# Two layers of attention on one core: the opening's instructions re-ordered, with 14 turns of the identity ahead of the first product

## The chip, the cores and the metric

The kernel runs on one core of a Trainium2 chip. The core has five engines with an instruction queue each: TensorE (matrix products into PSUM; PE in the profile, PEld for its weight loads), VectorE (DVE), ScalarE (ACT), GpSimd (POOL) and SyncE (SP, which here only issues transfers). Each works through its own queue in order, and an instruction that waits holds up all that is queued behind it on its engine. The metric is the device time of one execution in microseconds; lower is better.

## What is computed

Two layers over 1024 latent tokens and 256 context tokens of width 1024: layer 0 with windowed attention, layer 1 with latent attention. The change concerns the first steps of layer 0: the adaLN vector, the norm of every token, and the product with the columns of `w_in` that give the values.

```python
m = jax.nn.silu(cond) @ w + bias               # shift, scale, gate of the layer
hx = rms_norm(x, norm_g[i]) * (1.0 + scale_x[:, None]) + shift_x[:, None]
hc = rms_norm(ctx, norm_g[i]) * (1.0 + scale_c) + shift_c
q, k, v, g = jnp.split(h @ w_in, [...], axis=-1)
```

After the second layer the latent tokens go through a last `rms_norm`. All is in 32-bit floats; a product is made of three TensorE products, with each operand split in a top half (`hi`, rounded) and what is left (`lo`): hi with hi, hi with lo, lo with hi.

## The kernel before

**The opening** (lines 822 to 1056) makes `hT`, the normed, scaled and turned tokens, and at once multiplies them with the first block of `w_in` (`wt[0]`, the values). It cuts the 1280 tokens in five parts `p` of 256 (0 is the context) and the width of 1024 in four quarters `b` of 256, that is two `k` of 128 each. A *group* is a pair (p, b). `groups` lists their order: (0,0), (1,0), (2,0), (0,1), (1,1), (2,1), (3,0), (3,1), (4,0), (4,1), then all parts of quarters 2 and 3.

The order is written out by hand: the block is a `manual_schedule`, so every engine takes its instructions in the order of the code, and a step can't overtake another on its engine. (The planner `Plan`, which orders later stages by costs and due times, isn't on here.) The steps, by name:

- `x_load(p)` loads 256 tokens as two halves `j` of 128 (SP). `square(p)` (line 860, ScalarE, one Square with a sum per half), `norm(p)` (line 865, VectorE's mean, then a power of -0.5 on POOL) and `scale(p, j, engine)` (line 870) norm them in place.
- `ada_load(q, kk)`, `ada_mm(q, kk)`, `ada_copy()`, `ada_cols(q)` make the columns of scale and shift (`ada0.A`, `ada0.B`) of quarter q: 256 KB pieces of `ada_w` on SP, small products in the upper left of bank 6 (line 839), a copy by ScalarE (844), two products by `sel` (849), and three additions on VectorE (`set_cols`, 328 to 331). Four buffers hold the pieces, so a load of the next q waits for the `ada_mm` that reads its buffer.
- `turn(p, b, bank)` (line 877): four 128 x 128 transposes on TensorE into bank 5 or 7.
- `h_part(p, b, hi)` (line 884): per k one VectorE instruction (890) takes the bank times A plus B to `h`; then one cast (892) by ScalarE or POOL writes the top half of both k.
- `h_low(p, b, eng)` (line 895): h minus the top half, on VectorE or POOL.
- `v_part(p, b)` (line 899): the group's products: eight with the top half (906), then four with the low half (911), summed in PSUM bank p.
- `w0_load(i)`, `w0_cut(i)` (lines 923, 927): a quarter of `wt[0]`, and its split: top on ScalarE or POOL, low on POOL.
- `make(i)` (line 936): `turn`, `h_part` and `h_low` of group i.

Two buffers hold `h` (`hr`), and `PB` is the whole of PSUM in eight banks: 0 to 4 take the five parts' sums, 3 and 4 the thrown-away squares of parts 0 to 2 as well, 5 and 7 the turns, 6 the adaLN. The opening ends about 70 us after the start with the copies of the values (`v_out`) and the first products of the next block. In the last opening of the kernel, that of layer 1, lines 1464 and 1465 apply scale and shift with ScalarE on one half of a bank and VectorE on the other:

```python
nc.scalar.activation(h[:, 1], ps[:, 1], AF.Identity, bias=sb[:, 1], scale=sa[:, 1])
nc.vector.tensor_scalar(h[:, 0], ps[:, 0], sa[:, 0], sb[:, 0], ALU.mult, ALU.add)
```

Of the kernel before, what the change touches and what calls it, by code (L numbers as in the profile page):

```python
# [14 lines left out]
AF = mybir.ActivationFunctionType  # L15
ALU = mybir.AluOpType
# [4 lines left out]
D = 1024  # L21
# [5 lines left out]
EPS = 1e-6  # L27
# [190 lines left out]
def kernel(ctx: ExitStack, tc: tile.TileContext, t, out, dbg=None):  # L218
    plan = Plan()
    nc = Recorder(tc.nc, plan)  # L220
# [75 lines left out]
    mhalf = sm(1)  # L296
# [538 lines left out]
    def ada_mm(q, kk):  # L835
        for k in range(2):
            for a in range(2):
                r = 64 * k + 32 * a
                nc.tensor.matmul(
                    PA[r : r + 2, 0:256], sc[:, 2 * kk + k, :], aw[q, kk][:, k, a], start=kk == 0, stop=kk == 3  # L840
                )

    def ada_copy():
        nc.scalar.copy(am[0:98], PA[0:98, 0:256])

    def ada_cols(q):
        for j in range(2):
            o = PA[:, 256 + 34 * j : 290 + 34 * j]
            nc.tensor.matmul(o, am[0:98, j * 128 : j * 128 + 128], sel[0:98], start=True, stop=True)
        m = shp(PA[:, 256:512], 2, 34)  # L850
        ada0.set_cols(m[:, :, 32:34], 1, q, 2)
        ada0.set_cols(m[:, :, 0:2], 0, q, 2)
# [4 lines left out]
        for j in range(2):  # L857
            load(out=xn[p][0][:, j], in_=src[j * 128 : j * 128 + 128, :])

    def square(p):  # L860
        junk = V[:, 8:10].rearrange("p a b c -> p (a b c)") if p > 2 else PB[:, 3:5, :].rearrange("p a b -> p (a b)")
        for j in range(2):
            nc.scalar.activation(junk, xn[p][0][:, j], AF.Square, accum_out=xn[p][1][:, j : j + 1])

    def norm(p):
        _, sq, st = xn[p]
        nc.vector.tensor_scalar(st[:, 0:2], sq[:, 0:2], 1.0 / D, EPS, ALU.mult, ALU.add)
        nc.gpsimd.tensor_tensor(st[:, 2:4], st[:, 0:2], mhalf.to_broadcast([128, 2]), ALU.pow)

    def scale(p, j, eng):  # L870
        x, r = xn[p][0][:, j], xn[p][2][:, 2 + j : 3 + j]
        if eng is nc.scalar:
            nc.scalar.activation(x, x, AF.Copy, scale=r)
        else:
            eng.tensor_scalar_mul(x, x, r)

    def turn(p, b, bank):
        tbank[p, b] = ps = shp(PB[:, bank, :], 2, 256)
        for kk in range(2):
            for j in range(2):  # L880
                c0 = (2 * b + kk) * 128
                nc.tensor.transpose(ps[:, kk, j * 128 : j * 128 + 128], xn[p][0][:, j, c0 : c0 + 128], ident)

    def h_part(p, b, hi=nc.scalar.copy):
        w = 1 if p == 0 else 0
        ps, h = tbank[p, b], shp(hr.next(), 2, 256)
        for kk in range(2):
            k = 2 * b + kk
            sa, sb = ada0.A[:, k, w : w + 1], ada0.B[:, k, w : w + 1]
            nc.vector.tensor_scalar(h[:, kk], ps[:, kk], sa, sb, ALU.mult, ALU.add)  # L890
        ks = slice(2 * b, 2 * b + 2)
        hi(hT[p][:, 0, ks, :], h)
        hs[p, b] = h

    def h_low(p, b, eng=nc.gpsimd):
        ks = slice(2 * b, 2 * b + 2)
        eng.tensor_sub(hT[p][:, 1, ks, :], hs[p, b], hT[p][:, 0, ks, :].bitcast(F32))

    def v_part(p, b):
        h, W = hT[p], wt[0]  # L900
        for j in range(2):
            js = slice(j * 128, j * 128 + 128)
            o = PB[:, p, j * 256 : j * 256 + 256]
            for k in (2 * b, 2 * b + 1):
                for s in range(2):
                    nc.tensor.matmul(o, h[:, 0, k, js], W[:, s, k, :], start=k == j == s == 0, stop=False)  # L906
        for j in range(2):
            js = slice(j * 128, j * 128 + 128)
            o = PB[:, p, j * 256 : j * 256 + 256]
            for k in (2 * b, 2 * b + 1):  # L910
                nc.tensor.matmul(o, h[:, 1, k, js], W[:, 0, k, :], start=False, stop=j == 1 and k == 7)
# [15 lines left out]
    def w0_cut(i, top=nc.scalar.copy):  # L927
        hi, lo = (wt[0][:, s, 2 * i : 2 * i + 2, :] for s in range(2))
        top(hi, w0[i])
        nc.gpsimd.tensor_sub(lo, w0[i], hi.bitcast(F32))  # L930
# [5 lines left out]
    def make(i):  # L936
        if i < NG:
            turn(*groups[i], (5, 7)[i % 2])
            h_part(*groups[i], nc.gpsimd.tensor_copy if i == 3 else nc.scalar.copy)
        if i < 9:  # L940
            h_low(*groups[i])
        elif 10 < i <= NG:
            h_low(*groups[i - 1], nc.vector if i % 2 or i in (14, 16) else nc.gpsimd)
        if i == 9:
            h_low(*groups[i])
# [20 lines left out]
    ada_mm(0, 3)  # L966
    ada_copy()
    ada_cols(0)
    for kk in range(4):
        ada_load(1, kk)  # L970
    x_load(3)
    w0_load(2)
    w0_load(3)
    w0_cut(0, nc.gpsimd.tensor_copy)
    h_part(0, 0, nc.gpsimd.tensor_copy)
    square(1)
    norm(1)
    h_low(0, 0, nc.vector)
    for j in range(2):
        scale(1, j, nc.vector)  # L980
    v_part(0, 0)
    turn(1, 0, 7)
    square(2)
    norm(2)
    h_part(1, 0)
    scale(2, 0, nc.vector)
    scale(2, 1, nc.scalar)
    w0_cut(1)
    for kk in range(2):
        ada_mm(1, kk)  # L990
    h_low(1, 0, nc.vector)
    v_part(1, 0)
    turn(2, 0, 5)
    ada_mm(1, 2)
    h_part(2, 0)
    h_low(2, 0, nc.vector)
    ada_mm(1, 3)
    ada_copy()
    turn(0, 1, 7)
    ada_cols(1)  # L1000
    x_load(4)
    for kk in range(4):
        ada_load(2, kk)
    v_part(2, 0)
    turn(1, 1, 5)
    h_part(0, 1, nc.gpsimd.tensor_copy)
    square(3)
    h_low(0, 1, nc.vector)
    norm(3)
    h_part(1, 1)  # L1010
    h_low(1, 1)
    for i in range(3, NG):
        p, q = groups[i]
        if i > 7:
            make(i + 2)
        if i == 3:
            scale(3, 0, nc.vector)
            scale(3, 1, nc.scalar)
        v_part(p, q)
        if i < 8:  # L1020
            make(i + 2)
        if i == 3:
            square(4)
            norm(4)
        if i == 5:
            scale(4, 0, nc.vector)
            scale(4, 1, nc.scalar)
            ada_mm(2, 0)
            ada_mm(2, 1)
            w0_cut(2)  # L1030
        if i == 6:
            ada_mm(2, 2)
            ada_mm(2, 3)
            ada_copy()
            w0_cut(3)
        if i == 7:
            ada_cols(2)
            for kk in range(4):
                ada_load(3, kk)
        if i == 9:  # L1040
            fetch(1)
        if i in (9, 11):
            ada_mm(3, i - 9)
            ada_mm(3, i - 8)
        if i == 11:
            ada_copy()
            load(out=cosa, in_=t["cos_a"])
            load(out=sina, in_=t["sin_a"])
        if i == 12:
            ada_cols(3)  # L1050
        if i > 15:
            v_out(p - 1)
        if i in (12, 14, 16):
            next_item()
# [444 lines left out]
    for k in range(8):  # L1499
        w0_cut1(k, nc.vector if k % 2 else nc.gpsimd)  # L1500
        if k % 2:
            b = k // 2
# [611 lines left out]
```

## Time and profile before

| | |
|---|---|
| runs shown | 1487.2, 1489.08, 1856.97 us; median 1489.08 |
| the profiled execution | 1487.75 us, with a span of 1485.6 us from first to last instruction |
| mean granted TensorE clock | 0.998 |
| the opening: TensorE busy, 0 to 20 us | 8.43 us |
| 20 to 45 us | 23.18 us of 25 |
| DMA queues busy, 10 to 35 us | 1.06 to 1.11 of their 16 engines |

A row of the timeline gives start and length in us from the span's start, engine, line, operation, what it writes and reads, and, in brackets, how long the engine had been idle before it and what ended that. Instructions of one kind in a row are merged (x8). Lengths of TensorE's instructions overlap, as they are pipelined, so its rate is read from start to start. A transpose or a 32-bit product of `ada_mm` may show as more than one record. A row by groups gives busy time, mean length in ns of one, and idle time. A row by stretches gives, per engine (PE, PEld, DVE, ACT, POOL), busy time and instructions, then the granted clock, the DMA share and GB/s.

### The profile page before, as it was taken

Reading aid. Unit: us, or ns where it says so; the run is one execution under the profiler, and the core shown is the slowest. Engines: PE = TensorE matmul, PEld = TensorE weight load, DVE = VectorE, ACT = ScalarE, POOL = GpSimd, SP = SyncE. Lnnn points to the kernel's source line nnn. Section 1 sums busy time; section 2 is a strip of 40 time slices with the busy share of each in tenths; the row PEclk is TensorE's granted clock in tenths of the full one; section 3 lists DMA queues with packets and bytes.
Section 4 is the critical chain, followed back from the end, with each engine's and each line's share of the span. In section 5 each row is a group of like instructions: output and inputs, shape, how many; then the busy total and the mean of one; then the engine's idle time right before and its main releaser. Section 6 shows DMA issues by size and latency. Waiting matters only on the chain.

```text
span 1485.6 us, 25066 instructions
## 1 busy us (share of the span) xinstructions
PE 1462.1 (98%) x9036; PEld 1186.8 (80%) x9036; DVE 1060.5 (71%) x2025; ACT 737.5 (50%) x1401; POOL 808.6 (54%) x735
## 2 busy tenths in 40 slices
PE   6999999999999999999999999999999999999998
PEld 4888888888888888889888888767777767866687
DVE  3787789648778888877988777666576466556764
ACT  4421222359888878877554432443454344444321
POOL 2563366356454444456300240798788788789371
PEclk9999999999999999999999999999999999999999
DMA  9545644573343333337344566011112212120442
GB/s 334 173 166 175 212 146 174 186 245 110 122 140 121 104 100 100 97 98 257 101 118 120 169 236 201 23 44 49 50 61 69 61 47 62 54 68 28 154 148 86
DMA packets 146964, 186.01 MB, mean 125 GB/s; under 512 B 12812, under 2 KB 100492, under 8 KB 146840
## 3 DMA queue, kind: packets, MB, share of 16 engines
q1 hardware_dynamic: 141864, 177.75, 37.9%
q10 hardware_dynamic: 4976, 6.66, 1.3%
q8 instruction: 71, 1.16, 0.3%
q14 instruction: 53, 0.43, 0.1%
HBM read 134.02 MB, written 46.15 MB: 121 GB/s over the span
## 4 chain that ended last, share of the span: by engine, by line
PE 90%; DVE 4%; DMA 2%; issue 1%; ACT 1%; POOL 0%; POOLq 0%; DVEq 0%; ACTq 0%
PE PB L285 14%; PE PB L286 14%; PE PB L287 14%; PE PB L1791 13%; PE PB L1814 9%; PE PB L737 5%; PE PB L1757 5%; PE PB L727 5%; PE PB L697 3%; PE PB L698 3%; DMA arena_f<-ada_w 1%; PE PB L1825 1%; PE PB L906 1%; DVE arena_r L281 1%; PE PB L756 1%
## 5 line engine op out<-in xcount | busy, mean ns | idle before, releaser
L285 PE MATMUL PB<-arena_r 128*128 128x512 f32 (+2 forms) x1200 | 439.4, 366 | 1.1 <-DVE arena_f L1239 1.1
L286 PE MATMUL PB<-arena_r 128*128 128x512 f32 (+2 forms) x1200 | 433.7, 361 | 0.0
L287 PE MATMUL PB<-arena_r 128*128 128x512 f32 (+2 forms) x1200 | 433.3, 361 | 0.0
L1807 POOL TENSOR_TENSOR arena_f<-arena_f 128x1024 f32<-128x1024 f32 x120 | 285.9, 2383 | 8.2
L285 PEld LDWEIGHTS PB<-arena_r 128*128 128x128 f32 x1200 | 226.3, 189 | 45.7 <-issue 9.0
L287 PEld LDWEIGHTS PB<-arena_r 128*128 128x128 f32 x1200 | 226.3, 189 | 33.5
L286 PEld LDWEIGHTS PB<-arena_r 128*128 128x128 f32 x1200 | 226.4, 189 | 32.1 <-POOL arena_r L281 0.6
L1791 PE MATMUL PB<-arena_r 64*128 64x512 f32 (+1 forms) x1600 | 229.3, 395 | 0.0
L1801 ACT ACTIVATE arena_f<-PB 128x1024 f32<-128x1024 f32 x160 | 164.5, 1028 | 111.7 <-PE PB L1791 84.9
L1763 DVE TENSOR_REDUCE krF<-PB 128x1 f32<-128x512 f32 (+1 forms) x264 | 166.9, 677 | 65.6 <-PE PB L1757 65.6
L1791 PEld LDWEIGHTS PB<-arena_r 64*128 64x128 f32 (+1 forms) x1600 | 178.2, 185 | 15.7 <-issue 5.2
L704 DVE CUSTOM_DVE_ANT_0 arena_f<-PB,arena_f,small 128x256 f32<-128x256 f32 (+1 forms) x288 | 148.1, 524 | 51.4 <-PE PB L698 32.8
L280 ACT CAST arena_r<-PB 128x512 fp32r<-128x512 f32 (+2 forms) x207 | 115.3, 563 | 113.2 <-PE PB L287 73.3
L281 DVE TENSOR_TENSOR arena_r<-PB,arena_r 128x512 fp32r<-128x512 f32 (+2 forms) x207 | 134.2, 660 | 35.1 <-ACT arena_r L280 34.4
L1814 PE MATMUL PB<-arena_f 128*64 128x512 f32 x640 | 146.0, 595 | 0.0
L281 POOL TENSOR_TENSOR arena_r<-arena_f,arena_r 128x512 fp32r<-128x512 f32 (+1 forms) x64 | 87.7, 1386 | 105.2 <-ACT arena_r L280 91.0
L280 ACT CAST arena_r<-arena_f 128x512 fp32r<-128x512 f32 (+1 forms) x142 | 82.3, 610 | 90.2 <-PE PB L287 27.8
L710 ACT ACTIVATE arena_f<-arena_f,small 128x640 f32<-128x640 f32 (+2 forms) x160 | 119.1, 745 | 15.8 <-DVE small L704 13.7
L507 DVE SCALAR_TENSOR_TENSOR arena_f<-arena_f,small 128x512 f32<-128x512 f32 x98 | 114.9, 1217 | 10.5 <-DMA arena_f<-ada_w 10.3
L737 PE MATMUL PB<-arena_r 128*128 128x512 f32 x336 | 118.7, 429 | 0.0
L1757 PE MATMUL PB<-arena_r 64*128 64x512 f32 (+1 forms) x768 | 113.9, 355 | 0.1
L727 PE MATMUL PB<-ident,arena_f 128*128 128x128 f32 x672 | 108.7, 272 | 0.1
(216 smaller groups left out, 2083.0 us busy)
## 6 DMA issues: line engine op xcount, KB each, us to landing
arena_f<-ada_w SPq DMA_DIRECT2D x96, 256.0 KB, 4.1
arena_r<-q_d SPq DMA_DIRECT2D x160, 128.0 KB, 2.8
arena_f<-a_w_in SPq DMA_DIRECT2D x40, 256.0 KB, 4.1
arena_f<-b_w_in SPq DMA_DIRECT2D x36, 256.0 KB, 3.3
arena_f<-x SPq DMA_DIRECT2D x16, 512.0 KB, 6.4
q_d<-arena_f SPq DMA_DIRECT2D x16, 512.0 KB, 3.0
arena_r<-qn_d SPq DMA_DIRECT2D x16, 512.0 KB, 5.1
g_d<-arena_f ACTq DMA_DIRECT2D x20, 256.0 KB, 4.1
```

The source lines that it names most:

```text
L280: nc.scalar.copy(hi, src)
L281: (lo_eng or nc.vector).tensor_sub(lo, src, hi.bitcast(F32))
L285: nc.tensor.matmul(o, ah, bh, start=first, stop=False)
L286: nc.tensor.matmul(o, al, bh, start=False, stop=False)
L287: nc.tensor.matmul(o, ah, bl, start=False, stop=last)
L727: nc.tensor.transpose(pt[:, h, :], self.Ps[h][:, ci * 128 : ci * 128 + 128], ident)
L737: nc.tensor.matmul(self.pv, V[:, self.chunks[ci], self.g, :], PT[:, s], start=ci == 0 and s == 0, stop=ci == self.m - 1 and s == 1,)
L1757: nc.tensor.matmul(bank[:, o : o + n], self.q[r, s, bs], k[r, 0, n0 : n0 + n], start=s == 0, stop=s == 2)
L1763: nc.vector.reduce_max(self.mxp[:, e, b : b + 1, i], bank[:, 0:n], AX.X)
L1791: nc.tensor.matmul(PB[:, b + e, :], k[r, s, cs], q[r, sq], start=i == 0, stop=i == 4)
L1807: eng.tensor_add(acc, acc, E)
L1814: nc.tensor.matmul(PB[r, 7, :], Vq[:, c, h, :], E[:, e], start=c == 0, stop=c == NT - 1)
```

## The change

The opening's order is written anew; what is computed stays the same. `square` and `norm` can take one half of a part. `turn` goes half by half (j outside, k inside), `v_part` by k and not by j, so that a group can start when the first k is there. `h_part` gets two more forms: with `hi=None` ScalarE applies scale and shift itself from PSUM to the top half, beside VectorE's own pass; with `parts=2` the cast is made per k. Fourteen turns of the identity into bank 2 stand between `ada_cols(0)` and the first product. Turns of later groups stand ahead of `v_part` of earlier ones, the four `ada_mm(2)` move behind group (3,1), and with them the turns of part 4.

```diff
-    def square(p):
+    def square(p, js=range(2)):
...
-        for j in range(2):
+        for j in js:
...
-    def norm(p):
+    def norm(p, j=0, n=2):
         _, sq, st = xn[p]
-        nc.vector.tensor_scalar(st[:, 0:2], sq[:, 0:2], 1.0 / D, EPS, ALU.mult, ALU.add)
-        nc.gpsimd.tensor_tensor(st[:, 2:4], st[:, 0:2], mhalf.to_broadcast([128, 2]), ALU.pow)
+        nc.vector.tensor_scalar(st[:, j : j + n], sq[:, j : j + n], 1.0 / D, EPS, ALU.mult, ALU.add)
+        nc.gpsimd.tensor_tensor(st[:, 2 + j : 2 + j + n], st[:, j : j + n], mhalf.to_broadcast([128, n]), ALU.pow)
...
     def turn(p, b, bank):
         tbank[p, b] = ps = shp(PB[:, bank, :], 2, 256)
-        for kk in range(2):
-            for j in range(2):
+        for j in range(2):
+            for kk in range(2):
...
-    def h_part(p, b, hi=nc.scalar.copy):
+    def h_part(p, b, hi=nc.scalar.copy, parts=1):
...
             nc.vector.tensor_scalar(h[:, kk], ps[:, kk], sa, sb, ALU.mult, ALU.add)
+            if hi is None:
+                nc.scalar.activation(hT[p][:, 0, k], ps[:, kk], AF.Identity, bias=sb, scale=sa)
+            elif parts == 2:
+                hi(hT[p][:, 0, k], h[:, kk])
         ks = slice(2 * b, 2 * b + 2)
-        hi(hT[p][:, 0, ks, :], h)
+        if hi and parts == 1:
+            hi(hT[p][:, 0, ks, :], h)
...
     def v_part(p, b):
         h, W = hT[p], wt[0]
-        for j in range(2):
-            js = slice(j * 128, j * 128 + 128)
-            o = PB[:, p, j * 256 : j * 256 + 256]
-            for k in (2 * b, 2 * b + 1):
+        for k in (2 * b, 2 * b + 1):
+            for j in range(2):
+                js = slice(j * 128, j * 128 + 128)
+                o = PB[:, p, j * 256 : j * 256 + 256]
...
     def make(i):
         if i < NG:
             turn(*groups[i], (5, 7)[i % 2])
-            h_part(*groups[i], nc.gpsimd.tensor_copy if i == 3 else nc.scalar.copy)
+            h_part(*groups[i])
...
     ada_cols(0)
+    for _ in range(14):
+        nc.tensor.transpose(PB[:, 2, 0:128], ident, ident)
...
-    h_part(0, 0, nc.gpsimd.tensor_copy)
-    square(1)
-    norm(1)
+    h_part(0, 0, nc.gpsimd.tensor_copy, 2)
+    square(1, [0])
+    norm(1, 0, 1)
     h_low(0, 0, nc.vector)
-    for j in range(2):
-        scale(1, j, nc.vector)
+    square(1, [1])
+    norm(1, 1, 1)
+    scale(1, 0, nc.vector)
+    scale(1, 1, nc.vector)
     v_part(0, 0)
     turn(1, 0, 7)
     square(2)
-    norm(2)
-    h_part(1, 0)
+    norm(2, 0, 1)
+    h_part(1, 0, None)
+    norm(2, 1, 1)
+    h_low(1, 0, nc.vector)
     scale(2, 0, nc.vector)
     scale(2, 1, nc.scalar)
-    w0_cut(1)
-    for kk in range(2):
-        ada_mm(1, kk)
-    h_low(1, 0, nc.vector)
+    w0_cut(1, nc.gpsimd.tensor_copy)
+    ada_mm(1, 0)
     v_part(1, 0)
+    ada_mm(1, 1)
     turn(2, 0, 5)
+    h_part(2, 0, None)
+    h_low(2, 0, nc.vector)
     ada_mm(1, 2)
-    h_part(2, 0)
-    h_low(2, 0, nc.vector)
     ada_mm(1, 3)
     ada_copy()
     turn(0, 1, 7)
+    turn(1, 1, 5)
     ada_cols(1)
...
     v_part(2, 0)
-    turn(1, 1, 5)
-    h_part(0, 1, nc.gpsimd.tensor_copy)
+    h_part(0, 1, None)
     square(3)
     h_low(0, 1, nc.vector)
-    norm(3)
-    h_part(1, 1)
-    h_low(1, 1)
+    h_part(1, 1, nc.gpsimd.tensor_copy)
     for i in range(3, NG):
         p, q = groups[i]
         if i > 7:
             make(i + 2)
+        v_part(p, q)
         if i == 3:
+            turn(2, 1, 7)
+            h_part(2, 1, None)
+            norm(3)
+            h_low(1, 1, nc.vector)
+            h_low(2, 1, nc.vector)
             scale(3, 0, nc.vector)
             scale(3, 1, nc.scalar)
-        v_part(p, q)
-        if i < 8:
-            make(i + 2)
-        if i == 3:
+        if i == 4:
+            turn(3, 0, 5)
+            h_part(3, 0, None)
+            h_low(3, 0)
             square(4)
+        if i == 5:
+            turn(3, 1, 7)
+            h_part(3, 1, nc.gpsimd.tensor_copy)
             norm(4)
-        if i == 5:
+            h_low(3, 1, nc.vector)
             scale(4, 0, nc.vector)
             scale(4, 1, nc.scalar)
-            ada_mm(2, 0)
-            ada_mm(2, 1)
             w0_cut(2)
-        if i == 6:
-            ada_mm(2, 2)
-            ada_mm(2, 3)
+        if i == 7:
+            for kk in range(4):
+                ada_mm(2, kk)
             ada_copy()
+            make(8)
+            make(9)
+            ada_cols(2)
             w0_cut(3)
-        if i == 7:
-            ada_cols(2)
             for kk in range(4):
                 ada_load(3, kk)
```

## The prediction

> **What bounds the kernel now.** I read the busy times first, then busy time by stage.
>
> ```profile
> span 1485.6 us, 25066 instructions
> PE 1462.1 (98%) x9036; PEld 1186.8 (80%) x9036; DVE 1060.5 (71%) x2025; ACT 737.5 (50%) x1401; POOL 808.6 (54%) x735
> ```
> ```profile
> 45.00:1470.00 1425.00, 1421.40 (x8733) 1157.54 (x8733) 1035.24 (x1965) 712.26 (x1355) 790.14 (x711) 1.00 0.38 120
> 0.00:45.00 45.00, 31.61 (x243) 20.89 (x243) 19.48 (x47) 22.85 (x39) 17.02 (x21) 0.96 0.92 314
> ```
>
> From 45 us on TensorE is busy for 1421.4 of 1425 us, and the change touches nothing there but an order of work that hides under it. All that can move lies in the first 45 us, of which TensorE is busy for 31.6. So I follow TensorE's own rows through that stretch (start, length, what ended an idle time before it).
>
> ```profile
> 13.71 1.11 PE L882 MATMUL PB<-ident,arena_f 128*128 128x128 f32 x4
> ...
> 16.02 0.63 PE L849 MATMUL PB<-small,arena_f 98*128 98x34 f32 x4 [0.53 <-ACT arena_f L844]
> 18.94 2.08 PE L906 MATMUL PB<-arena_r 128*128 128x256 f32 x8 [2.28 <-POOL arena_r L892]
> ...
> 21.67 0.71 PE L882 MATMUL PB<-ident,arena_f 128*128 128x128 f32 x4
> ...
> 25.92 0.60 PE L882 MATMUL PB<-ident,arena_f 128*128 128x128 f32 x4
> 26.45 1.04 PE L839 MATMUL PB<-arena_f,small 128*2 128x256 f32 x16
> ...
> 28.53 0.63 PE L849 MATMUL PB<-small,arena_f 98*128 98x34 f32 x4 [0.45 <-ACT arena_f L844]
> ...
> 31.46 1.22 PE L906 MATMUL PB<-arena_r 128*128 128x256 f32 x8 [0.35 <-POOL arena_r L892]
> ...
> 35.76 0.60 PE L882 MATMUL PB<-ident,arena_f 128*128 128x128 f32 x4
> ...
> 43.91 0.64 PE L911 MATMUL PB<-arena_r 128*128 128x256 f32 x4
> 44.39 0.60 PE L882 MATMUL PB<-ident,arena_f 128*128 128x128 f32 x4
> ...
> 47.09 0.60 PE L882 MATMUL PB<-ident,arena_f 128*128 128x128 f32 x4
> 47.45 1.19 PE L906 MATMUL PB<-arena_r 128*128 128x256 f32 x8
> 48.48 0.64 PE L911 MATMUL PB<-arena_r 128*128 128x256 f32 x4
> 49.05 1.04 PE L839 MATMUL PB<-arena_f,small 128*2 128x256 f32 x16
> ```
>
> Start to start at full clock, `turn` costs 47.45 - 47.09 = 0.36 us (0.09 a turn), a group's eight high products (L906) 1.03 and its four low ones (L911) 0.57 with what follows, about 0.5 alone; four `ada_mm` (L839, x16) take 1.0. The idle times before 45 us are a single large one (2.28 us, on POOL's cast of the first values) and then small ones. TensorE is only just ahead of the engines that feed it, so those decide what the new order does.
>
> The clock has one gap in the same place:
>
> ```profile
> 11.67:15.08 3.41, 3.41 (x22) 1.01 (x20) 0.49 (x1) 0.00 (x0) 0.13 (x1) 1.00 1.08 377
> 15.08:18.49 3.41, 1.05 (x12) 0.52 (x4) 1.39 (x5) 2.48 (x4) 1.96 (x3) 1.00 1.03 409
> 18.49:21.90 3.41, 2.96 (x14) 2.96 (x15) 2.38 (x5) 2.48 (x6) 1.70 (x3) 0.50 1.08 351
> 21.90:25.31 3.41, 3.10 (x27) 1.49 (x26) 2.35 (x4) 1.85 (x3) 0.57 (x1) 1.00 1.11 354
> ```
>
> A stretch of 3.41 us with TensorE 31% busy is followed by one at a granted 0.50, and a busy one ends it. The first group and the next `turn` took 18.94 to 22.3 there, 3.4 us, against 1.03 + 0.5 + 0.36 = 1.9 at full clock.
>
> **The change, part by part.** Durations not seen in the rows above:
>
> ```profile
> L868 POOL TENSOR_TENSOR small<-small 128x2 f32<-128x2 f32 x5 | 4.0, 795 | 12.8 <-DVE small L867 12.7
> L763 POOL CAST arena_r<-arena_f 128x256 fp32r<-128x256 f32 x39 | 15.5, 398 | 2.5
> L897 POOL TENSOR_TENSOR arena_r<-arena_f,arena_r 128x512 fp32r<-128x512 f32 x9 | 12.2, 1362 | 7.0 <-ACT arena_r L892 7.0
> L897 DVE TENSOR_TENSOR arena_r<-arena_f,arena_r 128x512 fp32r<-128x512 f32 x11 | 7.6, 693 | 1.4 <-POOL arena_r L892 0.7 <-ACT arena_r L892 0.7
> L892 ACT CAST arena_r<-arena_f 128x512 fp32r<-128x512 f32 x18 | 11.2, 620 | 21.2 <-DVE arena_f L890 21.2
> L863 ACT ACTIVATE arena_r<-arena_f 128x1024 fp32r<-128x1024 f32 x4 | 4.2, 1058 | 0.1
> L873 ACT ACTIVATE arena_f<-arena_f,small 128x1024 f32<-128x1024 f32 x3 | 3.4, 1148 | 0.0
> ```
> ```profile
> 17.22 0.99 DVE L890 TENSOR_SCALAR arena_f<-PB,small 128x256 f32<-128x256 f32 x2
> ...
> 20.21 1.42 DVE L875 TENSOR_SCALAR arena_f<-arena_f,small 128x1024 f32<-128x1024 f32 x2 [0.60 <-POOL small L868]
> ...
> 29.73 1.00 DVE L890 TENSOR_SCALAR arena_f<-PB,small 128x256 f32<-128x256 f32 x2
> ```
>
> *The 14 turns* stand behind `ada_cols(0)`, from 16.6 on: 14 x 0.09 = 1.3 us, to 17.9 (at half clock, by the row at 21.67, 0.16 to 0.18 each, to 19.1). The first product is ready at 18.2, so at full clock they cost nothing. If they keep the clock they save up to 3.4 - 1.9 = 1.5 us, but only if the next item is ready. It isn't (below), so I count 0.
>
> *The first values in two halves.* The two L890 start at 17.22; the first ends half way, near 17.75, POOL casts 256 columns in 0.40, and the product may start at 18.2 instead of 18.94; at full clock it ends, with its low half, at 19.9.
>
> *norm(1) in two.* Two POOL powers of 0.8 in place of one: 18.7 to 19.5 to 20.3; then `scale(1,1)` on VectorE (0.7) ends at 21.05 and `turn(1,0)` at 21.5. In before it ended at 21.67 + 0.71 = 22.4. This, not the clock, is what TensorE waits for: gain 0.9.
>
> *h_part with None: VectorE and ScalarE each turn PSUM into values and top half.* This is the core. It replaces two L890 (1.00) and a cast (0.62), 1.65 us with the hand-overs, by two pairs of reads of one PSUM bank. The same pair exists later in the kernel:
>
> ```profile
> 677.49 1.00 ACT L1464 ACTIVATE arena_f<-PB,small 128x256 f32<-128x256 f32 x2
> 678.07 1.00 DVE L1465 TENSOR_SCALAR arena_f<-PB,small 128x256 f32<-128x256 f32 x2 [1.41 <-ACT arena_f L1464]
> ...
> 690.59 0.57 ACT L1464 ACTIVATE arena_f<-PB,small 128x256 f32<-128x256 f32 x1
> ...
> 691.19 0.54 DVE L1465 TENSOR_SCALAR arena_f<-PB,small 128x256 f32<-128x256 f32 x1 [0.69 <-ACT arena_f L1464]
> ```
>
> There ScalarE reads one half of a bank and VectorE the other, they write different halves, and yet VectorE stands idle (1.41 and 0.69 us) until ScalarE's read of that bank ends, and starts 0.02 us behind. So the two take turns: 0.54 + 0.56 + 0.54 + 0.56 and three hand-overs are 2.3 us. Bounds for the pair are thus 1.1 us (side by side) and 2.3; I take 2.3. The low half (L897 on VectorE) comes 0.7 later, 3.0 behind the turn instead of 2.35, and VectorE's second read is stuck behind ScalarE's first, with `norm`, `h_low` and `scale` queued behind it.
>
> *The order of the queues, hand to hand with these prices* (before, then after, for the same work done):
>
> - `turn(1,0)` done 21.5; values by ScalarE at 22.6 and 23.8, low at 24.5, `scale(2,0)` 25.2, `scale(2,1)` 25.35 (ScalarE, 1.15, behind a power that is now its own). Group (1,0) ends 25.05, `ada_mm(1,1)` 25.55; `turn(2,0)` at 25.55 (before 25.92): ahead by 0.4.
> - Its values end on ScalarE at 28.5. `ada_copy` is queued behind them, 28.85; `turn(1,1)` needs the same bank 5 and stands on TensorE ahead of `ada_cols(1)`: 28.9 (before 28.53). Behind by 0.4, with `turn(1,1)` done.
> - L890 of (0,1) follows 1.2 behind `ada_cols(1)` as in the row at 29.73, at 30.1; ScalarE's halves at 31.2 and 32.4; group (0,1) ends 33.65 (before 33.0). ScalarE then has square(3), 2.35, to 34.8.
> - `turn(2,1)` 34.0 to 34.3. Its pair alternates with square(3) ahead of it: done 36.6. `h_low(1,1)` stands behind it on VectorE, 36.75, `h_low(2,1)` 37.35, `scale(3,0)` 38.05; group (1,1) waits for its low half until 36.8, and `turn(3,0)`, which stands ahead of group (2,1) on TensorE, for the scale: 38.1 (before 35.76). Behind by 2.3.
> - Group (2,1) to 39.6; the values of (3,0) end 41.05, POOL's low half (1.36) 42.4, its cast for (3,1) 43.0; group (3,1) ends 44.8. Before it ended at 43.91 + 0.5 = 44.4, with `ada_mm(2)` (2.0) and `turn(4,0)` (0.36) done. Behind by 2.8.
> - `ada_mm(2)` to 46.75, and only now `turn(4,0)`: L890 1.0, cast 0.62, POOL's low half 1.36, some 3.5 us with the turn, under which lie two turns, `ada_cols(2)` and eight products, 2.5. Group (4,1) ends 52.7, before 49.05: behind by 3.65.
>
> From there on TensorE is the bound as before, since `fetch(1)` moves by the same amount and its values are used 18 us later. Transfers stay where they are to 25 us (the q=1 pieces of `ada_w` go out as `ada_mm(0)` frees their buffers, which nothing changes); those that follow start with `ada_mm` and `w0_cut` and are wanted later too.
>
> **Sum:** 1487.75 (the profiled execution's own time) + 3.65 = 1491.4. The median of the runs shown, 1489.08, lies 1.3 above the profiled execution, the lowest, 1487.2, 0.55 below it; that spread is in the range.
>
> **Rivals.** *Side by side* (1487.3): if the two engines read the bank together, each of the five pairs ends 1.2 earlier. `turn(3,0)` then comes at about 35.0, group (3,1) is ahead by 1.3, and the bare chain of (4,0) gives back about 0.9: ahead by 0.4. For it: ScalarE's and VectorE's x2 rows overlap where they are on different banks. Against: both waits quoted. *A second cold stretch* (1492.9): the sum leaves TensorE thin from 35 to 38.4 us (0.5 of low products, a turn, the end of a group, under 50%). If the clock is dropped at a share above that (the rows only show that 31% does it), the next 3.4 us run at half: groups (2,1) and (3,0) pay up to 1.5 more, by the 3.4 against 1.9 above. It decides only on the slow side. *The turns don't hold the clock* (1491.9): then the first product runs half cold from 18.5 and ends near 21.2, `turn(1,0)` near 22.0, 0.5 later than in the sum. For this speaks that nothing here shows how turns count; against it that the stretch before 15.08 holds the four turns at 13.71 and is followed by 1.00. The Trainium skill's "TensorE: Matmul & The Clock Gate", Part 4 (PE-mode transpose), says that transposes don't count as busy for the clock in the same way; that is this rival.
>
> **How the numbers follow.** Chances: the forecast 0.58, side by side 0.15, a second cold stretch 0.15, turns that don't hold the clock 0.12. Powers of 0.7 to 1.2 move the sum by -0.1 to +0.4 and POOL's contended low halves by 0.3; errors of hand-overs over some twenty steps about 1; executions spread by -0.5 to +1.3. So the likeliest case alone spans 1489.3 to 1493.6, and with part of the rivals the range is 1487.0 to 1494.2. A measurement of this kernel tells about 2% from no change, 30 us; every case here lies within 7, so within 2% has 0.98.
>
> **What would show it.** Right: ScalarE's affine reads and VectorE's alternate by bank, 2.3 us a pair; TensorE waits on ScalarE or VectorE before `turn(1,1)` or `ada_cols(1)`, before `turn(3,0)` and in groups (4,0); 1.00 granted at 18.5 to 21.9; `ada_mm(3)` starts near 52.7. Wrong: pairs that overlap, or `ada_mm(3)` before 50.

## The result, and the profile after

| | before | changed |
|---|---|---|
| median, 9 runs each | 1488.35 us | 1492.49 us (1491.86 to 1493.43) |
| ratio, with its 95% interval | | 1.0029 [1.0019, 1.0039] |
| the profiled execution | 1487.75 us | 1493.12 us |
| `ada_mm(3)` starts | 49.05 us | 53.80 us |

The change costs 4.1 us; a repeat beside other kernels below gave 5.0, with a ratio of 1.0035 [1.0021, 1.0049]. The prediction was 1491.4, from 1487.0 to 1494.2. (One of before's nine runs, 1856.97, is a disturbed one; the ratio leaves it out.)

Span and busy times first, then the two stages, then four stretches of 3.41 us, the first two with the cuts of the kernel before, the last two cut where this execution's clock changed (PE, PEld, DVE, ACT, POOL, then the granted clock, DMA share, GB/s):

```profile
span 1491.0 us, 25106 instructions
PE 1465.9 (98%) x9050; PEld 1188.9 (80%) x9050; DVE 1064.6 (71%) x2030; ACT 739.0 (50%) x1404; POOL 807.6 (54%) x737
```
```profile
0.00:45.00 45.00, 31.23 (x210) 20.35 (x211) 20.71 (x49) 21.57 (x37) 13.91 (x21) 0.96 0.83 283
45.00:1470.00 1425.00, 1420.10 (x8756) 1155.65 (x8755) 1036.48 (x1966) 713.55 (x1356) 792.22 (x713) 1.00 0.39 121
15.08:18.49 3.41, 2.82 (x23) 2.42 (x22) 2.72 (x9) 2.74 (x5) 2.37 (x4) 1.00 1.02 402
18.49:21.90 3.41, 2.50 (x17) 1.13 (x16) 2.05 (x5) 2.27 (x5) 1.53 (x2) 1.00 1.10 355
...
35.44:38.85 3.41, 1.93 (x13) 1.33 (x12) 2.56 (x5) 1.71 (x2) 1.07 (x1) 1.00 0.65 206
38.85:42.26 3.41, 3.41 (x18) 3.41 (x17) 1.09 (x2) 2.12 (x4) 0.92 (x1) 0.50 0.01 2
```

From 45 us on TensorE is as full as before (1420.1 of 1425 against 1421.4), so the loss lies in the opening: the changed kernel's profiled execution is 4.75 us behind before's when `ada_mm(3)` starts. The stretch that before had at 0.50, from 18.49, now has 1.00. But a new one at 0.50 has come at 38.85, behind a stretch with TensorE busy for 1.93 of 3.41 us.

TensorE's own rows of the changed kernel (start, length, and in brackets the idle time before it and what ended it; L911 and L916 are now the high and low products, L839 is `ada_mm`, L882 `turn`):

```profile
14.54 0.63 PE L849 MATMUL PB<-small,arena_f 98*128 98x34 f32 x4 [0.51 <-ACT arena_f L844]
15.01 1.73 PE L975 MATMUL PB<-ident 128*128 128x128 f32 x14
17.33 1.21 PE L911 MATMUL PB<-arena_r 128*128 128x256 f32 x8 [0.59 <-POOL arena_r L894]
...
19.24 0.44 PE L882 MATMUL PB<-ident,arena_f 128*128 128x128 f32 x2
20.43 0.44 PE L882 MATMUL PB<-ident,arena_f 128*128 128x128 f32 x2 [0.75 <-DVE small L867]
...
28.30 0.66 PE L882 MATMUL PB<-ident,arena_f 128*128 128x128 f32 x4 [0.85 <-ACT arena_r L892]
28.79 0.53 PE L849 MATMUL PB<-small,arena_f 98*128 98x34 f32 x4
...
36.72 0.74 PE L916 MATMUL PB<-arena_r 128*128 128x256 f32 x4 [0.87 <-DVE arena_r L902]
38.08 0.83 PE L882 MATMUL PB<-ident,arena_f 128*128 128x128 f32 x4 [0.62 <-DVE arena_f L875]
38.66 1.90 PE L911 MATMUL PB<-arena_r 128*128 128x256 f32 x8
...
44.03 1.22 PE L911 MATMUL PB<-arena_r 128*128 128x256 f32 x8 [0.27 <-POOL arena_r L897]
...
45.65 1.91 PE L839 MATMUL PB<-arena_f,small 128*2 128x256 f32 x32
...
53.80 1.04 PE L839 MATMUL PB<-arena_f,small 128*2 128x256 f32 x16
```

Read it down to the waits: the second half of `turn(1,0)` at 20.43 (for `scale(1,1)` behind its power), `turn(1,1)` at 28.30 (for ScalarE's last read of bank 5), the low half of (1,1) at 36.72, `turn(3,0)` at 38.08 (for `scale(3,0)`). Then the eight products of (2,1) take 1.90 us instead of 1.2: that is the new stretch at 0.50. The first pair of reads of one bank, on VectorE and on ScalarE:

```profile
20.91 0.54 DVE L890 TENSOR_SCALAR arena_f<-PB,small 128x256 f32<-128x256 f32 x1 [0.47 <-PE PB L882]
22.09 0.54 DVE L890 TENSOR_SCALAR arena_f<-PB,small 128x256 f32<-128x256 f32 x1 [0.64 <-ACT arena_r L892]
```
```profile
21.49 0.57 ACT L892 ACTIVATE arena_r<-PB,small 128x256 fp32r<-128x256 f32 x1 [0.95 <-DVE arena_f L890]
22.67 0.56 ACT L892 ACTIVATE arena_r<-PB,small 128x256 fp32r<-128x256 f32 x1 [0.61 <-DVE arena_f L890]
```

Four reads, none beside another: 20.91 to 23.23 is 2.3 us. VectorE's second read waits 0.64 us for ScalarE's first, though the two write different buffers and the second read looks at another half of the bank.

### The profile page after: what moved, and what is told of

Same layout as the page of the kernel before. It is cut to its first block, busy times and chain, and to the rows that moved or that the text cites. A ratio compares the mean times of both kernels' runs of the same rounds, so it can differ in the third digit from the quotient of the medians.

```text
span 1491.0 us, 25106 instructions
## 1 busy us (share of the span) xinstructions
PE 1465.9 (98%) x9050; PEld 1188.9 (80%) x9050; DVE 1064.6 (71%) x2030; ACT 739.0 (50%) x1404; POOL 807.6 (54%) x737
## 4 chain that ended last, share of the span: by engine, by line
PE 90%; DVE 4%; issue 2%; DMA 1%; ACT 1%; POOL 1%; SPq 0%; POOLq 0%; DVEq 0%; ACTq 0%
PE PB L285 14%; PE PB L286 14%; PE PB L287 14%; PE PB L1807 13%; PE PB L1830 9%; PE PB L737 5%; PE PB L1773 5%; PE PB L727 5%; PE PB L697 3%; PE PB L698 3%; PE PB L911 1%; PE PB L1841 1%; DVE arena_r L281 1%; PE PB L882 1%; PE PB L916 1%
## 5 line engine op out<-in xcount | busy, mean ns | idle before, releaser
L1807 PE MATMUL PB<-arena_r 64*128 64x512 f32 (+1 forms) x1600 | 227.2, 395 | 0.0
L710 ACT ACTIVATE arena_f<-arena_f,small 128x640 f32<-128x640 f32 (+2 forms) x160 | 119.1, 745 | 15.5 <-DVE small L704 13.9
L1773 PE MATMUL PB<-arena_r 64*128 64x512 f32 (+1 forms) x768 | 111.8, 355 | 0.1
```

What stands on the lines that cost most here:

```text
L1773: nc.tensor.matmul(bank[:, o : o + n], self.q[r, s, bs], k[r, 0, n0 : n0 + n], start=s == 0, stop=s == 2)
L1807: nc.tensor.matmul(PB[:, b + e, :], k[r, s, cs], q[r, sq], start=i == 0, stop=i == 4)
```

## The experiments

Theory A is the prediction's: the two engines take turns on a bank, and that and the order of the queues cost the time. B: the passes overlap well enough, and the cost lies in the new order alone. C: the clock decides (turns that don't hold it, or a second cold stretch). All runs in one table; "before" is the median of the kernel before measured beside it, and the last columns are rows of TensorE in the profiled execution.

| kernel | median us | before | ratio [95%] | `ada_cols(0)` | `ada_mm(3)` |
|---|---|---|---|---|---|
| e1_cast_per_k | 1489.68 | 1487.72 | 1.0014 [1.0005, 1.0023] | 15.48 | 50.20 |
| e2_no_turns | 1493.3 | 1487.72 | 1.0037 [1.0025, 1.0050] | 14.83 | 54.27 |
| e3_turns_alone | 1487.37 | 1487.72 | 0.9998 [0.9990, 1.0007] | 14.77 | 48.32 |
| e4_pairs_alone | 1493.58 | 1487.72 | 1.0039 [1.0026, 1.0052] | 14.79 | 53.71 |
| e5_two_banks | 1488.75 | 1487.71 | 1.0010 [1.0001, 1.0019] | 15.24 | 50.15 |
| e6_new_head_old_tail | 1489.52 | 1487.71 | 1.0014 [1.0006, 1.0023] | 14.96 | 50.57 |
| e7_four_pairs | 1490.41 | 1487.71 | 1.0018 [1.0009, 1.0027] | 14.89 | 51.14 |
| e8_change_again | 1492.68 | 1487.71 | 1.0035 [1.0021, 1.0049] | 14.36 | 53.69 |
| e9_mended | 1488.1 | 1487.6 | 1.0003 [0.9994, 1.0012] | 15.17 | 49.82 |
| e10_square_first | 1491.25 | 1487.6 | 1.0026 [1.0015, 1.0036] | 14.67 | 52.42 |
| e11_more_turns | 1492.71 | 1487.6 | 1.0034 [1.0022, 1.0047] | 14.46 | 54.42 |
| e12_part4_early | 1486.87 | 1487.69 | 0.9991 [0.9982, 1.0000] | 14.95 | 48.77 |

The start of `ada_mm(3)` puts the kernels nearly in the order of their times: the opening hands its delay on almost one to one, as the prediction assumed. `ada_cols(0)` comes at 14.4 to 15.5 in all of these and at 16.02 only in the profile of before, but its place doesn't order the times: in several of these profiles TensorE then waits for a piece of `ada_w` some 7 us later.

**e1: a cast per k in place of ScalarE's own pass from PSUM** (changed kernel, all five groups).

```diff
-    h_part(1, 0, None)
+    h_part(1, 0, nc.scalar.copy, 2)
... (the same for (2,0), (0,1), (2,1), (3,0))
```

> The changed kernel with the five pairs on one bank taken away: in groups (1,0), (2,0), (0,1), (2,1) and (3,0) VectorE alone reads the bank, and ScalarE casts the top half from SBUF, k by k. All else, the order and the 14 turns, stays. Theory A (the alternation on one bank is the loss): a pair of 2.3 us becomes 1.4 (0.54 + 0.37, the second k half hidden), turn(3,0) comes near 35.5 instead of 38.1, no stretch under 60% busy is left, and the time falls by 3 to 4.5 us below the changed kernel, to 1488 to 1489.5. Theory B (the order is the loss: turn(3,0) ahead of group (2,1), the low halves behind the next part's values, part 4 late): at most 1.5 us are won, 1491 or above.

The loss shrinks to 2.0 us, so by 2.2 to 3.0, at or below the low end of Theory A's 3 to 4.5 and above B's 1.5. TensorE's rows of it:

```profile
35.97 0.83 PE L882 MATMUL PB<-ident,arena_f 128*128 128x128 f32 x4 [1.22 <-DVE arena_f L875]
...
50.20 1.04 PE L839 MATMUL PB<-arena_f,small 128*2 128x256 f32 x16
```

`turn(3,0)` comes 2.1 us earlier than in the changed kernel, and waits the longer for its scale: the pass from PSUM is the larger part of the loss. What is left is put down to the order here; e9 and e12 test that.

**e2: the changed kernel without the 14 turns.**

```diff
-    for _ in range(14):
-        nc.tensor.transpose(PB[:, 2, 0:128], ident, ident)
```

> The changed kernel without the 14 turns of the identity. Theory A (what the clock gives ahead of the first product is taken by the wait for scale(1,1) and by the pieces of ada_w): the same within 0.7 us, though the granted clock falls to 0.50 behind the first columns and the first group takes some 3 us. Rival (the turns are worth their clock): slower by 1.2 to 1.7 us, and the loss of the rest is then larger than 4.

```profile
17.61 1.21 PE L911 MATMUL PB<-arena_r 128*128 128x256 f32 x8 [2.14 <-POOL arena_r L894]
18.79 1.11 PE L916 MATMUL PB<-arena_r 128*128 128x256 f32 x4
...
20.71 0.69 PE L882 MATMUL PB<-ident,arena_f 128*128 128x128 f32 x2 [0.38 <-DVE small L867]
```

Without the turns the clock drops: the four low products take 1.11 us, against 0.74 at full clock. Yet the second half of `turn(1,0)` starts 5.88 us behind `ada_cols(0)` (20.71 - 14.83), and in the changed kernel 5.89 (20.43 - 14.54): it still waits for `scale(1,1)`, only 0.38 us instead of 0.75. So the cold products lie under the wait, as the prediction had it. By the times, each taken from the kernel before measured beside it, the turns save 0.6 to 1.4 us (5.6 above before, against 5.0 and 4.1), which the intervals don't tell from nothing.

**e3: the kernel before with the 14 turns**, behind its `ada_cols(0)`.

> The kernel before with the 14 turns alone. Theory A: the first group is done 1.0 to 1.5 us earlier at full clock, but turn(1,0) waits for scale(1,1), which ended at 21.63 against 21.67 before, and later for the pieces of ada_w: faster by 0 to 0.7 us. Rival (the cold stretch of before costs its 1.5 us): faster by 1.2 us or more.

```profile
11.67:15.08 3.41, 2.89 (x23) 1.05 (x21) 0.00 (x0) 0.37 (x1) 0.80 (x2) 1.00 1.06 391
15.08:18.49 3.41, 2.36 (x21) 2.12 (x21) 2.24 (x7) 2.71 (x5) 1.96 (x3) 1.00 1.02 400
18.49:21.90 3.41, 2.65 (x23) 1.65 (x21) 2.25 (x6) 1.88 (x4) 1.50 (x2) 1.00 1.10 350
```

The turns hold the clock: with them the stretch to 18.49 has TensorE busy for 2.36 us instead of 1.05, and 1.00 follows instead of 0.50. The time moves by -0.35 us, within its interval. Here too the work behind them waits for the scales (0.42 and 0.34 us before the turns of (1,0)). The Trainium skill's "TensorE: Matmul & The Clock Gate", Part 4 (PE-mode transpose), says that a transpose doesn't count as busy for the clock in the same way; these rows disagree for a turn of 32-bit data, so the rival built on it fell.

**e4: the kernel before with the pass from PSUM in the five groups**, its order kept.

```diff
             nc.vector.tensor_scalar(h[:, kk], ps[:, kk], sa, sb, ALU.mult, ALU.add)
+            if hi is None:
+                nc.scalar.activation(hT[p][:, 0, k], ps[:, kk], AF.Identity, bias=sb, scale=sa)
...
-    h_part(1, 0)
+    h_part(1, 0, None)
```

> The kernel before with nothing but the pairs: h_part of groups (1,0), (2,0), (0,1), (2,1) and (3,0) lets ScalarE apply scale and shift from the bank beside VectorE, in the order of before. Theory A (alternation): the top half is there 2.3 instead of 1.65 us behind each turn; on the path of (2,0) with ada_copy behind it, of (0,1) and of (3,0) this is 0.65 each, so slower by 1.3 to 2.5 us. Theory B (the order is the loss): the same within 0.6 us.

A miss: 5.9 us, more than the whole change. ScalarE's, VectorE's and TensorE's rows tell why:

```profile
32.59 1.05 ACT L863 ACTIVATE arena_r<-arena_f 128x1024 fp32r<-128x1024 f32 x1
...
36.03 0.62 ACT L895 CAST arena_r<-arena_f 128x512 fp32r<-128x512 f32 x1 [1.13 <-DVE arena_f L890]
```
```profile
34.94 0.17 DVE L867 TENSOR_SCALAR small<-small 128x2 f32<-128x2 f32 x1 [1.53 <-ACT arena_r L863]
35.01 0.99 DVE L890 TENSOR_SCALAR arena_f<-PB,small 128x256 f32<-128x256 f32 x2
```
```profile
33.56 0.64 PE L914 MATMUL PB<-arena_r 128*128 128x256 f32 x4
34.04 0.60 PE L882 MATMUL PB<-ident,arena_f 128*128 128x128 f32 x4
36.71 1.21 PE L909 MATMUL PB<-arena_r 128*128 128x256 f32 x8 [2.07 <-ACT arena_r L895]
```

`square(3)` stands behind the pair of (0,1) in ScalarE's queue and starts at 32.59 (28.38 in before). `norm(3)` on VectorE (34.94) waits for it with the values of (1,1) queued behind it, so their cast comes at 36.03 and TensorE stands for 2.07 us. My expectation had priced the pair and not what is queued behind it.

**e5: the changed kernel with the second k of each of the five turns in another bank** (2, 3 or 4, which are free then).

```diff
-    def turn(p, b, bank):
-        tbank[p, b] = ps = shp(PB[:, bank, :], 2, 256)
+    def turn(p, b, bank, other=None):
+        ps = shp(PB[:, bank, :], 2, 256)
+        tbank[p, b] = ps = [ps[:, 0], ps[:, 1] if other is None else PB[:, other, 0:256]]
...
-    turn(1, 0, 7)
+    turn(1, 0, 7, 2)
... (the same for the four others, with bank 3 or 4)
```

> The changed kernel, with ScalarE's own pass from PSUM kept, but the second k of each of the five turns (1,0), (2,0), (0,1), (2,1), (3,0) put in another bank (2, 3 or 4, free there). Theory A (two engines take turns on one bank): VectorE's second L890 now follows its first by 0.5 and not by 1.18, ScalarE's second pass ends 1.7 instead of 2.3 us behind the turn, and the time falls by 1 to 2.5 us below the changed kernel of the same call. Rival (the two are kept apart by something else, an operand they share or PSUM as a whole): 1.18 stays, and the time with it, within 0.5 us.

The rows of VectorE, of ScalarE, and of TensorE:

```profile
21.46 1.00 DVE L891 TENSOR_SCALAR arena_f<-PB,small 128x256 f32<-128x256 f32 x2 [0.36 <-PE PB L883]
```
```profile
22.04 1.02 ACT L893 ACTIVATE arena_r<-PB,small 128x256 fp32r<-128x256 f32 x2 [0.88 <-DVE arena_f L891]
```
```profile
35.92 0.83 PE L883 MATMUL PB<-ident,arena_f 128*128 128x128 f32 x4 [0.62 <-DVE arena_f L875]
...
40.38 1.21 PE L912 MATMUL PB<-arena_r 128*128 128x256 f32 x8
```

Same instructions, same order: VectorE's two reads now stand back to back, ScalarE's follow half a read behind, and the pair takes 21.46 to 23.06, 1.6 us instead of 2.3. The kernel gains 3.9 us on the changed one measured beside it (1488.75 against 1492.68; the ratios' intervals don't meet), more than the 1 to 2.5 expected, and is 1.0 above before. This is the test that tells A from B: the bank's turn-taking is most of the loss. Two things are in it that this run doesn't take apart: the pairs are shorter, and a bank comes free earlier (`turn(1,1)`, which waits 0.85 us for ScalarE's last read of bank 5 in the changed kernel, doesn't wait here). The Trainium skill's "PSUM — Partial Sum Buffer", section "PSUM bank collisions raise a hardware error", says that two engines mustn't read one bank in the same partitions at once, even at other addresses, and that a dependency is put between them; the rows agree, with 0.64 us of waiting per pair on VectorE and none with two banks. What ends that wait in the rows is ScalarE's instruction, so they show an order that the program keeps; what the bank would do with two reads at once no run here shows.

**e6: e1's head with before's loop** from group (1,1) on, so that `turn(3,0)` and part 4 stand where they stood.

> The casts per k of the first run, and from group (0,1) on the order of the kernel before: turn(3,0) behind the low half that needs nothing of it, low halves on POOL, ada_mm(2) in pairs between the groups, part 4 turned early. If the order of the tail is the rest of the loss (turn(3,0) waiting 1.2 us for its scale, part 4 late with some 0.9): 2 to 3 us below the first run, at or up to 1 us below the kernel before. If the loss were in the head (norm in two, the turns, the pieces of ada_w): as slow as the first run, 1 to 2 us above the kernel before.

A miss: 1.8 us, the same as e1.

```profile
34.76 0.74 PE L916 MATMUL PB<-arena_r 128*128 128x256 f32 x4 [0.95 <-POOL arena_r L902]
...
36.86 1.21 PE L911 MATMUL PB<-arena_r 128*128 128x256 f32 x8 [0.90 <-ACT arena_r L897]
```

The old tail assumes a ScalarE that is free early. In the new head `square(3)` stands behind the casts of (0,1), so the low half of (1,1) and the cast of (2,1) are late, and TensorE waits for these in place of the scale.

**e7: e4 without the pass for (0,1)**, whose values POOL casts as in before.

> The kernel before with ScalarE's own pass in four groups, (1,0), (2,0), (2,1) and (3,0), and POOL's cast kept in (0,1), so that square(3) isn't pushed behind a pass of ScalarE that waits for ada_cols(1). If most of the 5.9 us that five pairs cost came from that queue (square(3) at 32.6 instead of 28.4, norm(3) and the values of (1,1) behind it): 1 to 2.5 us above the kernel before. If each pair costs about the same: 4 to 5 us.

2.7 us, just above the 1 to 2.5 expected, against 5.9 with it. One pair, with its own longer reads and by standing ahead of `square(3)`, cost 3.2 us; the four others 2.7 together.

**e8: the changed kernel again**, measured beside e5 to e7.

> The changed kernel once more, for comparison in one call: 3.5 to 5 us above the kernel before. Executions with a second cold stretch behind turn(3,0) should lie about 1 us above those without.

5.0 us above before. Its profile too has the stretch at a low clock behind `turn(3,0)`: 37.90 to 43.91 from that turn to group (3,1).

**e9: e1 with ScalarE's queue mended**: `square(3)` ahead of (0,1), whose values POOL casts per k, as it does for (1,1); `norm(3)`, the scales and the low half of (1,1) earlier.

```diff
-    h_part(0, 1, nc.scalar.copy, 2)
     square(3)
+    h_part(0, 1, nc.gpsimd.tensor_copy, 2)
+    norm(3)
     h_low(0, 1, nc.vector)
-    h_part(1, 1, nc.gpsimd.tensor_copy)
+    h_part(1, 1, nc.gpsimd.tensor_copy, 2)
+    h_low(1, 1)
...
-            norm(3)
-            h_low(1, 1, nc.vector)
-            h_low(2, 1, nc.vector)
             scale(3, 0, nc.vector)
             scale(3, 1, nc.scalar)
+            h_low(2, 1, nc.vector)
```

> The order of the change with what the runs so far point to: casts per k from SBUF in place of the five pairs, those of (0,1) and (1,1) on POOL, so that ScalarE does square(3) while ada_cols(1) is still awaited; norm(3) and scale(3) earlier; h_low(1,1) back on POOL. If ScalarE's queue in front of square(3) is what the first and sixth run still lose: turn(3,0) waits no longer for its scale (1.2 us in the first run) and the time is that of the kernel before or up to 1.5 us below it. If the rest lies elsewhere (the head, or part 4 late): 1 to 2 us above the kernel before, as in those two.

0.5 us above before, which the measurement doesn't tell from no change. Its profile shows a wait that I put there myself, in ScalarE's rows and in TensorE's:

```profile
30.16 1.06 ACT L863 ACTIVATE arena_r<-arena_f 128x1024 fp32r<-128x1024 f32 x1 [1.36 <-DMA arena_f<-x]
```
```profile
32.16 0.74 PE L916 MATMUL PB<-arena_r 128*128 128x256 f32 x4 [0.92 <-DVE arena_r L902]
```

The second half of part 3's tokens lands only at 30, `norm(3)` waits for its square, and `h_low(0,1)` is queued behind `norm(3)` on VectorE.

**e10: the changed kernel with only `square(3)` ahead and (0,1) cast by POOL per k.**

```diff
-    h_part(0, 1, None)
     square(3)
+    h_part(0, 1, nc.gpsimd.tensor_copy, 2)
```

> The changed kernel with one pair less and no more: the values of (0,1) are cast by POOL, per k, and square(3) stands ahead of them on ScalarE. The other four pairs stay. Theory A, with the pair's own 0.9 (2.3 against 1.4) and a ScalarE free for the pair of (2,1): 1 to 2 us below the changed kernel. If a pair costs nothing beside the order of the rest: the same as the change within 0.5 us.

3.65 us above before, so 0.5 to 1.3 better than the changed kernel (4.1 and 5.0), where 1 to 2 were expected, with intervals that overlap. `turn(3,0)` starts 22.66 us behind `ada_cols(0)` (37.33 - 14.67) against 23.54, and no stretch at 0.50 follows it.

**e11: the changed kernel with 8 more turns of the identity ahead of `turn(3,0)`**, to keep the clock there.

```diff
         if i == 4:
+            for _ in range(8):
+                nc.tensor.transpose(PB[:, 5, 0:128], ident, ident)
             turn(3, 0, 5)
```

> The changed kernel with eight more turns of the identity, into bank 5 ahead of turn(3,0), in the idle time that ends with its scale (0.6 us in one profile, with 0.9 ahead of it). If the second cold stretch is from the thin 3.4 us before it: no granted 0.50 behind turn(3,0), the first group there takes 1.2 and not 1.9 us, and the median falls by 0.3 to 1.2 us below the change. If turns don't count for the clock: the stretch stays, and the time is the same or 0.3 us longer.

```profile
38.56 1.03 PE L1035 MATMUL PB<-ident 128*128 128x128 f32 x8
39.44 0.73 PE L882 MATMUL PB<-ident,arena_f 128*128 128x128 f32 x4
39.92 1.19 PE L911 MATMUL PB<-arena_r 128*128 128x256 f32 x8
...
43.94 0.74 PE L916 MATMUL PB<-arena_r 128*128 128x256 f32 x4 [0.62 <-POOL arena_r L902]
44.52 1.19 PE L911 MATMUL PB<-arena_r 128*128 128x256 f32 x8
```

In this profile the drop behind `turn(3,0)` is gone (by steps of 3.41 us from its own change of clock, the stretch ahead, 35.90 to 39.31, has TensorE busy for 2.54 us and not 1.93): the products of (2,1) take 1.19 us instead of 1.90. From `turn(3,0)` to group (3,1) it takes 44.52 - 39.44 = 5.08 us (5.18 in e10), against 44.03 - 38.08 = 5.95 with the drop (6.01 in e8). So the drop costs 0.8 to 0.9 us, and not the 1.5 of the rival: the low half of (3,0) on POOL holds the next group up in any case (the row at 43.94). The eight turns take 39.44 - 38.56 = 0.88, but nearly all of that in the wait for the scale: from the low products of (1,1) to `turn(3,0)` it takes 1.46 us with them and 1.36 without. Yet the median doesn't fall: 5.1 us above before, against 4.1 and 5.0. Why is open. The intervals, 1.5 to 1.9 us to either side, don't tell a gain of 0.8 from none, and it isn't known which executions of the changed kernel have the drop. (This profiled execution also has a stretch at a low clock from 22.24 to 25.65; its time, 1493.13, is 0.4 above the kernel's median.)

**e12: e9 with the wait mended and part 4 early**: `norm(3)` behind `h_low(0,1)`, `square(4)` in halves and `norm(4)` earlier, the turns of (4,0) and `ada_mm(2)` one group earlier.

```diff
     square(3)
+    square(4, [0])
     h_part(0, 1, nc.gpsimd.tensor_copy, 2)
-    norm(3)
     h_low(0, 1, nc.vector)
+    norm(3)
...
-        if i == 7:
+        if i == 6:
+            make(8)
             for kk in range(4):
                 ada_mm(2, kk)
             ada_copy()
-            make(8)
+        if i == 7:
             make(9)
```

> The ninth run with the two waits that its profile still shows taken out: norm(3) stands behind h_low(0,1) (group (0,1) waited 0.9 us for it, as VectorE stood at norm(3) until x of part 3 had landed and been squared), and part 4 is made before it is late: square(4) in ScalarE's two gaps, scale(4) earlier, turn(4,0) and the four ada_mm(2) ahead of group (3,1), turn(4,1) behind it. If these are what keeps the new order from its lead (1.4 us at group (0,1), 0.3 at turn(3,0), then 0.8 behind at ada_mm(3)): ada_mm(3) starts near 48.4 instead of 49.8 and the time is 1 to 2 us below the kernel before. If the lead is lost elsewhere or square(4) waits for its x: no better than the ninth run.

```profile
40.72 1.91 PE L839 MATMUL PB<-arena_f,small 128*2 128x256 f32 x32
...
48.77 1.04 PE L839 MATMUL PB<-arena_f,small 128*2 128x256 f32 x16
```

The lowest median of all, 0.8 us below before, with a ratio of 0.9991 [0.9982, 1.0000] that just reaches 1. Less than the 1 to 2 expected: `ada_mm(3)` starts at 48.77 and not near 48.4. It keeps the new head (per-k casts, halves of squares and norms, the 14 turns), without the pass from PSUM.

## Why the prediction was right, and where its sizes were off

1. *What bounds.* Right. Between the two profiled executions, 4.75 of the 5.37 us are there at `ada_mm(3)` (the 0.6 behind it isn't explained), and the start of `ada_mm(3)` nearly follows the time over all the kernels.
2. *The turns.* Right in effect: they hold the clock and save little (0.35 us alone, 0.6 to 1.4 in the change, neither told from nothing), because `turn(1,0)` waits for `scale(1,1)` (e2, e3). They are dearer than I took them, 1.73 us for 14 by the length of the row, so up to 0.12 each instead of 0.09, and in the changed kernel's profile still end 0.6 us before the first product is ready.
3. *The pair on one bank.* Right to the tenth: 2.3 us, taken from the two rows of the other layer's opening. e5 shows that the bank is the reason. The rival in which the engines read side by side fell, and its price was off too: it took 1.1 us for a pair, and with two banks it is 1.6, as ScalarE reads each k behind VectorE; e5 is 1.0 above before, not 0.4 ahead.
4. *The chain.* By the start times of its steps it held to 38 us: `ada_copy` 28.14 (predicted 28.5), `ada_cols(1)` 28.79 (28.9), `turn(2,1)` 33.64 (34.0), the low half of (1,1) 36.72 (36.8), `turn(3,0)` 38.08 (38.1). The head ran up to 0.9 us ahead of it (first product 17.33 against 18.2), as `ada_cols(0)` came 1.5 us earlier in this execution; that was gone by 29 us. So the agreement to the tenth is in part luck: from `ada_cols(0)` to `turn(3,0)` it took 23.54 us, and the prediction had 38.1 - 16.02 = 22.1.
5. *Behind 38 us* the forecast was too small: group (3,1) ends near 45.65 where I had 44.8, and `ada_mm(3)` starts at 53.80 instead of 52.7. The step that failed is the assumption that the clock stays at 1.00 there. I had it as a rival with 0.15, and it happened in both profiles of the changed kernel and in that of e2. Its price was 0.8 to 0.9 us, not 1.5; the other 0.25 lie between group (3,1) and `ada_mm(3)`. With the drop the forecast would have been 1492.2 or 1492.3, beside 1492.49 and 1492.68 measured. But whether it comes in every execution isn't known, so neither is whether the medians have it. Of the nine timed runs the three with a mean clock of 0.998 are the slowest (1493.12 to 1493.43, the profiled one among them), and the six with 0.999 or 1.000 took 1491.86 to 1492.65. In e8's five runs there is no such order: 1491.8 and 1492.68 at 0.998, 1492.55 to 1493.66 at 0.999.
6. *ScalarE's queue.* The prediction had `square(3)` end at 34.8 behind the pair of (0,1), as a link of the chain and without a price of its own. e4, e7 and e10 give one: 3.2 us in before's order, and 0.9 up to `turn(3,0)` in the new one, where more stands between.

By the runs the loss of 5.0 us in e8 splits so: 3.9 the bank's turn-taking, with the cold stretch that its lateness brings on (e5 against e8); the remaining 1.0 is put down to the order. Undoing the pass and mending the order gives 0.5 above before (e9); with e9's wait mended and part 4 earlier it is 0.8 below (e12), though the intervals of the two overlap. These parts aren't additive to the tenth: e10 gives 0.5 to 1.3 with `square(3)` ahead and the pair of (0,1) gone, and its profile is also without the cold stretch.

## What to carry to other kernels

In these runs ScalarE and VectorE, on the two halves of one PSUM bank, worked one after the other; put the halves in two banks before judging whether splitting the work is worth it. When an engine is given more to do, price what is queued behind it and who waits for that: one early pair ahead of a square cost about as much as the four other pairs together (3.2 and 2.7 us). And a clock kept high is worth only as much as the next instruction is ready earlier.

## What the runs showed of the hardware that was not expected

- The clock drops without a wholly idle stretch. By steps of 3.41 us from where the clock changed in the same execution, 1.73 us of TensorE (51%, e11) and 1.91 to 1.94 us (56 to 57%, e8, the changed kernel, e2) were followed by 0.50; before, 31% was. In e4 2.28 us (67%) were followed by 1.00, but so were 1.90 us (56%), as the second row shows by its clock:

```profile
32.33:35.74 3.41, 1.90 (x14) 1.66 (x14) 1.50 (x4) 2.54 (x5) 0.56 (x1) 1.00 1.10 351
35.74:39.15 3.41, 2.28 (x17) 2.08 (x18) 1.93 (x4) 2.50 (x4) 1.43 (x2) 1.00 0.72 229
```

  So at 56 to 57% of busy time, as the profile counts it, both happened, and this share alone doesn't say when the clock drops.
- Turns of the identity count towards it (e3, e11).
- A small instruction can grow fourfold and more beside another engine's. VectorE's addition of `set_cols`, 0.16 us in before's profile, took 0.70 here while POOL split the weights (rows of VectorE, then of POOL, of the changed kernel):

```profile
15.46 0.70 DVE L331 SCALAR_TENSOR_TENSOR small<-small 128x4 f32<-128x4 f32 x1
```
```profile
14.86 1.28 POOL L935 TENSOR_TENSOR arena_r<-arena_f,arena_r 128x512 fp32r<-128x512 f32 x1
```

  It ends at 16.16, POOL's at 16.14. In eleven other profiles too it starts beside that instruction of POOL, at other distances, takes 0.39 to 0.86 us, and ends 0.01 to 0.03 us behind it; where POOL had ended (before, e1) it took 0.16. VectorE's addition of line 328, at 15.27 in the changed kernel, took 0.16 in the midst of the same instruction of POOL. So this one addition waits for POOL to end; no run was made to take the two apart.
